# Weights split ahead of time in the first layer, kept in DRAM, and loaded ready made by the attention stage

## The chip, the cores and the metric

One core of a Trainium2 chip runs the kernel. The metric is the device time of one execution in microseconds (us), taken as the median of several runs. Engines are named as in the profile: PE (TensorE, matrix products; PEld its weight loads), DVE (VectorE), ACT (ScalarE), POOL (GpSimd) and SP (SyncE, which issues DMA transfers here). POOL issues DMA transfers as well, on a queue of its own; the accumulating ones must come from it. SBUF is the on-chip memory, PSUM the banks that PE writes to, DRAM the memory outside.

## The reference

Two layers of a decoder on 1024 tokens of width 1024, all in float32:

```
for i in (0, 1):
    h = rmsnorm(x, norm_mixer[i])
    if i == 0: mix = short_conv(h, w_in, conv_w, w_out)          # gated convolution, width 3
    else:      mix = attention(h, w_qkv, gains, sinks, w_o)      # window of 128, 16 query heads, 4 key heads
    x = x + mix
    h = rmsnorm(x, norm_ffn[i])
    x = x + (silu(h @ w_gate) * (h @ w_up)) @ w_down             # channel mixer, inner width 2816
```

The attention takes 128-query blocks against the block's own and the preceding 128 keys, with RMS norms on the heads of queries and keys, a linear distance bias (ALiBi), and one learned sink logit for each head.

## The kernel before, in words

**Products.** A float32 weight is split into two parts, `hi` (the value rounded to the engine's fast format, F32R) and `lo` (the rest). A product of tiles is three matmuls of 128x128 by 128x512: hi by the operand's high part, hi by its low part, lo by its high part. A split is two instructions on a 128x512 piece (a *granule*): a cast that makes `hi` and a subtraction that makes `lo`. The large products also use a Strassen-like scheme with seven products of half the size (k = 0 to 6) in the place of eight. For four of the seven, the weights are sums of quarters of the matrix. These sums are made in DRAM: plain copies on SP's queue fill a DRAM tile (`s4`, called `q_sums`, for the query weights; `s2_...` for the down projection), and a chain of four accumulating DMA transfers on POOL's queue (`added_sums`, line 901) forms the sums, each transfer waiting for the one before.

**The order of the work.** In the channel mixers and the first mixer, a list called `line` holds every instruction with a planned time: `line.at(t, f)` files a step, `line.work` files matmuls that take 0.2265 us each, and at the end all are issued in order of planned time. So the plan sets only the order on each engine; what an instruction waits for, it waits for when the program runs. In the attention stage the order is a string, one letter for each kind of step (`ORDER`), repeated 64 times, once for each pair of heads and block of queries, and `plan(d, f)` files a step d repetitions later.

**The stages, in order of time.** The convolution layer; its channel mixer (`channel_mixer(0, ...)`: gate and up products with 22 units, of which the last 18, the *steady* ones, take 7 x 12 matmuls or about 19 us each, then the down product from `begin` on); the attention layer; its channel mixer. In the first channel mixer's steady part, from about 400 to 743 us, SP loads two 512 KB weight tiles for each unit (WR and WH, lines 1478 and 1482), ACT and DVE split granules 13 us ahead of their use (lines 937 and 938), ACT and DVE empty PSUM banks (lines 1374 to 1436), and POOL's queue carries the stores of the hidden values (`h`, lines 1431 and 1456 to 1458) and the accumulations for the sums that later stages need, planned 9 us apart. SBUF tiles X0 and X2 hold nothing during the steady units.

**The attention layer.** The first 14 granules, for keys and the first pair of query tiles (`first_pairs`), and the values come first. The other 21 granules of query weights are *streamed* during the 64 repetitions: `load_granule(j)` loads 256 KB of raw weights, from `w_q` or, for sums, from `q_sums`; `split_granule(j + 1, pool, pool)` has POOL make both parts; `three(j, p, x)` makes the product (line 2048). Products of four of the seven kinds read operands that were stored in DRAM earlier (`q_ops`), through `load_operand` (512 KB each). Beside this, for each repetition, PE makes scores (line 2257), POOL the distances (line 2272), DVE the row maxima (`mx`, line 2284), ACT the exponents; POOL also splits queries (line 2216), output operands (line 2470) and a few small things. In the tail of this stage the product with the first half of the output weights runs (`w_o`, eight row tiles m, with the first EARLY = 4 blocks of each): its weights are loaded by `Weights.load` and split by ACT and POOL.

Of the kernel before, what the change touches and what calls it, by code (L numbers as in the profile page):

```python
# [15 lines left out]
P = 128  # L16
# [71 lines left out]
def trunk_kernel(ctx: ExitStack, tc: tile.TileContext, xT, small, w_in, w_out, w_q, w_v, w_o, w_gu, w_dn, out):  # L88
# [6 lines left out]
    def slot(tag, shape=(P, D), dtype=F32, bufs=1):  # L95
        uid[0] += 1
        return sb.tile(list(shape), dtype, tag=tag, name=f"{tag}_{uid[0]}", bufs=bufs)
# [737 lines left out]
    q_sums = tc.dram_tile((4, GROUP + 1, P, 5 * P), F32, name="s4")  # L835
    q_ops = tc.dram_tile((4, 4, P, D), F32, name="q_ops")
    xres = [tc.dram_tile((P, T), F32, name=f"xres{m}") for m in range(NK)]
    x_aside = {m: tc.dram_tile((P, T), F32, name=f"x_aside{m}") for m in (NK - 2, NK - 1)}
    first_sums = [tc.dram_tile((4, GROUP, P, 5 * P), F32, name=f"s1_{l}") for l in range(2)]
    down_sums = [[tc.dram_tile((4, P, (PAIRS + 1) * P), F32, name=f"s2_{l}_{u}") for u in range(GROUP)] for l in range(2)]  # L840
    hidden = [[tc.dram_tile((KINDS, 2, P, HALF), F32, name=f"h_{l}_{i}") for i in range(SLOTS)] for l in range(2)]
    lo_half, hi_half = slice(0, HALF), slice(HALF, T)

    class Line:
# [221 lines left out]
    def channel_mixer(layer, next_stage, src_of, operands, raw_tags, extra_tags, keep_tags, slots, begin_with=(), first_w=None, line=None, lead_in=None, before=None, follow=None):  # L1066
# [520 lines left out]
        if layer == 0:  # L1587
            first_added_sums(1, line, begin + 10.0, 18.0)
            for i, (u, n) in enumerate(((0, 2), (2, 2), (KEYS_AS_PAIR, 1))):
                dst = [q_sums[s, u : u + n][:, :, 0 : 4 * P] for s in range(4)]  # L1590
                parts = [w_q[e, u : u + n][:, :, r] for e in (0, 1) for r in (0, 1)]
                added_sums(dst, parts, line, steady_begins + 75.0 * i + 30.0, 9.0)
# [67 lines left out]
    def attention_layer():  # L1660
# [295 lines left out]
        halves_of = (lo_half, hi_half)  # L1956
        seq = [(KEYS_AS_PAIR, k) for k in KEY_ORDER] + [(u, k) for u in range(NK // 2) for k in QUERY_ORDER]
        n_first = 2 * KINDS
        rooms = {}
# [3 lines left out]
        def pair_rooms():  # L1963
            wr = slot("WR", (P, 2, 4 * P), bufs=2)
            rooms["held"] = slot("WR", (P, 2, HALF), bufs=2)
            rooms["spare"] = slot("WH", (P, 2, HALF), F32R, bufs=2)
            rooms["odd"] = slot("WH", bufs=2)
            wl = [slot("WL", (P, 2, 4 * P), F32R, bufs=2) for _ in range(2)]
            g0 = slot("G0", (P, 2, 4 * P))
            rooms["raws"] = [x[:, i] for x in (wr, g0) for i in (0, 1)]  # L1970
            rooms["grans"] = wl + [rooms["spare"], slot("G2", (P, 2, 4 * P), F32R)]
            rooms["banks"] = [bank(f"P{i}") for i in range(3)]

        def raw_room(j):
            return rooms["raws"][j % 4 if j < n_first else j % 2]

        def gran_room(j):
            return rooms["grans"][j % 4 if j < n_first - 1 else 2 if j == n_first - 1 else j % 2]

        def load_granule(j):  # L1980
            if j < len(seq):
                u, k = seq[j]
                src = {0: w_q[0, u][:, 0], 1: w_q[0, u][:, 1], 4: w_q[1, u][:, 1]}
                src = src[k] if k in src else q_sums[SUMS[k], u][:, 0 : 4 * P]
                nc.sync.dma_start(raw_room(j), src)
            elif j == len(seq):
                nc.sync.dma_start(raw_room(j).rearrange("p (k c) -> p k c", c=P), w_o[0][:, 0 : len(early), :])

# [62 lines left out]
        def first_pairs():  # L2051
# [61 lines left out]
            for j in range(n_first):  # L2113
# [31 lines left out]
                if j == 11:  # L2145
                    at(t + 0.75, first.squares0)
                    at(t + 0.8, keep_v, 0, 1)
            for j in range(n_first + 2):
                if j < n_first:
                    t = begins[j - 3 + (j == n_first - 1)] + 0.05 if j > 3 else begin + 14.0 + 2.4 * j  # L2150
                    at(t, split_granule, j, act, pool if j > 10 else dve)
                if j < 6:
                    at(begin + (2.0 + 1.2 * j if j < 4 else 5.5 + 2.4 * j), load_granule, j)
                else:
                    at(begins[j - (6 if j < n_first else 4)] + (0.02 if j <= n_first else 1.0), load_granule, j)
            at(begins[n_first - 1] + 0.05, split_granule, n_first, act, dve)
            at(begins[n_first - 1] + 1.0, split_granule, n_first + 1, act, pool)
            at(begins[n_first - 1] + 1.2, load_granule, n_first + 2)
            for n in range(4):
# [252 lines left out]
        def plan(d, f):  # L2412

            agenda.setdefault(pos["step"] + d, []).append(f)
# [91 lines left out]
        def work_of_pairs():  # L2506
            n = 0
            for j in range(n_first, len(seq)):
                u, k = seq[j]
                plan(0, lambda j=j: split_granule(j + 1, pool, pool) if j > n_first else None)  # L2510
                if j > n_first:
# [24 lines left out]
        with tc.manual_schedule(engines={E.PE, E.Activation, E.DVE, E.Pool, E.SP}):  # L2536
# [24 lines left out]
            for m in range(NK):  # L2561
                acc = Acc()
                work = product(acc, w, o_split, len(early))
                for k in range(len(early)):
                    if m + 1 < NK and k == 0:
                        w_next = Weights()
                        w_next.load(w_o[m + 1][:, 0 : len(early), :], 0, len(early))
                    if m == 2 and k == 0:
# [15 lines left out]
                    step(work, full=(k != REST or m in (2, 5)) and pos["n"] < NU + 3)  # L2584
                    if m + 1 < NK and k in (1, 2):
                        w_next.split(2 * (k - 1), 2, act, pool)
                run(work)
# [126 lines left out]
```

## Time and profile before

| | us |
|---|---|
| median of 3 runs | 1934.55 (1933.93 to 1935.43) |
| profiled execution | 1935.29 |
| its span, first to last instruction | 1933.4 |
| PE busy | 1912.8 |
| DVE, ACT, POOL busy | 1304.0, 898.0, 367.4 |

The clock granted to PE was 0.997 on average. In the profile's rows, `acc` and `P` are PSUM banks, `XS`, `A`, `G`, `WR`, `WH`, `WL` and `X` SBUF tiles, `s` and `h` DRAM tiles; `out<-in` names what an instruction writes and reads, with buffer numbers left out. L901 is a line of the kernel's source; lines of helpers (L937, L938: the two halves of a split) stand for many places. A wait row reads: engine and line that waited, what it waited for, total, number of times, longest.

### The profile page before, as it was taken

What the parts mean: (1) busy time and instruction counts of PE and PEld (TensorE: products, weight loads), DVE (VectorE), ACT (ScalarE), POOL (GpSimd) and SP (SyncE); (2) the same over time, 40 slices, a digit from 0 to 9 for tenths busy, and PEclk for the clock granted to TensorE, in tenths of its full rate; (3) what the DMA queues carried; (4) which work ended last, traced back from release to release, by engine and by line L of the source; (5) the groups of instructions that cost most, each with busy time, mean ns of one, the idle gap of its engine ahead of it and who ended that gap; (6) DMA issues with size and microseconds to landing.
All of it is one profiled execution on the core that took longest, in us unless ns stands there. A gap on an engine that the chain in (4) does not pass through costs nothing.

```text
span 1933.4 us, 25467 instructions
## 1 busy us (share of the span) xinstructions
PE 1912.8 (99%) x8981; PEld 1594.0 (82%) x8981; DVE 1304.0 (67%) x2257; ACT 898.0 (46%) x1762; POOL 367.4 (19%) x504
## 2 busy tenths in 40 slices
PE   9999999999999999999999999999999999999999
PEld 8888888888888888888887788888888888888887
DVE  8997877975665666556765677788665665665543
ACT  5543464623333334445457777655333333344441
POOL 0011231011211100000017888310111111100000
PEclk9999999999999999999999999999999999999999
DMA  8897595388888638986474562242674676468562
GB/s 316 249 256 148 132 250 157 113 272 213 226 249 227 169 120 307 321 251 191 139 255 160 172 209 79 63 171 71 218 216 131 209 187 169 129 235 281 195 229 99
DMA packets 155487, 376.22 MB, mean 195 GB/s; under 512 B 15456, under 2 KB 26848, under 8 KB 155360
## 3 DMA queue, kind: packets, MB, share of 16 engines
q1 hardware_dynamic: 119968, 265.25, 40.4%
q0 software_dynamic: 35248, 109.33, 23.5%
q8 instruction: 70, 1.15, 0.2%
q14 instruction: 57, 0.47, 0.1%
q10 hardware_dynamic: 144, 0.03, 0.0%
HBM read 301.93 MB, written 150.47 MB: 234 GB/s over the span
## 4 chain that ended last, share of the span: by engine, by line
PE 92%; POOL 3%; DVE 1%; ACT 1%; issue 1%; DMA 0%; POOLq 0%; DVEq 0%; ACTq 0%
PE acc L1004 16%; PE acc L1005 16%; PE acc L1007 16%; PE P L1004 10%; PE P L1007 10%; PE P L1005 10%; PE acc L171 2%; PE P L2048 2%; PE acc L2048 2%; POOL G L2216 1%; PE acc L175 1%; PE P L2313 1%; PE acc L1137 1%; PE acc L1139 1%; PE acc L1138 1%
## 5 line engine op out<-in xcount | busy, mean ns | idle before, releaser
L1004 PE MATMUL acc<-XS,G 128*128 128x512 f32 x926 | 360.4, 389 | 0.0
L1007 PE MATMUL acc<-XS,G 128*128 128x512 f32 x926 | 360.3, 389 | 0.0
L1005 PE MATMUL acc<-XS,G 128*128 128x512 f32 x926 | 360.2, 389 | 0.0
L1004 PE MATMUL P<-A,G 128*128 128x512 f32 x550 | 214.2, 389 | 0.4 <-DVE G L547 0.4
L1005 PE MATMUL P<-A,G 128*128 128x512 f32 x550 | 214.0, 389 | 0.0
L1007 PE MATMUL P<-A,G 128*128 128x512 f32 x550 | 214.0, 389 | 0.0
L1005 PEld LDWEIGHTS acc<-XS,G 128*128 128x128 f32 x926 | 173.8, 188 | 36.1
L1004 PEld LDWEIGHTS acc<-XS,G 128*128 128x128 f32 x926 | 173.8, 188 | 36.1
L1007 PEld LDWEIGHTS acc<-XS,G 128*128 128x128 f32 x926 | 173.8, 188 | 36.0
L1004 PE MATMUL acc<-A,G 128*128 128x512 f32 x442 | 172.1, 389 | 0.0
L1007 PE MATMUL acc<-A,G 128*128 128x512 f32 x442 | 172.0, 389 | 0.0
L1005 PE MATMUL acc<-A,G 128*128 128x512 f32 x442 | 171.9, 389 | 0.0
L938 DVE TENSOR_TENSOR G<-WR,G 128x512 fp32r<-128x512 f32 (+1 forms) x216 | 144.2, 668 | 30.0 <-ACT G L937 29.8
L938 DVE TENSOR_TENSOR G<-WL,G 128x512 fp32r<-128x512 f32 x168 | 115.0, 685 | 73.1 <-ACT G L937 73.1
L937 ACT CAST G<-WR 128x512 fp32r<-128x512 f32 (+1 forms) x216 | 130.4, 605 | 59.3 <-PE acc L1007 25.5
L937 ACT CAST G<-WH 128x512 fp32r<-128x512 f32 (+1 forms) x174 | 104.6, 601 | 85.0 <-PE acc L1007 41.8
L1339 ACT ACTIVATE G<-G 128x512 f32<-128x512 f32 x88 | 55.8, 634 | 159.1 <-DVE G L1436 152.9
L938 DVE TENSOR_TENSOR G<-WH,G 128x512 fp32r<-128x512 f32 (+1 forms) x174 | 115.5, 664 | 21.0 <-ACT G L937 20.9
L901 POOL DMA_DIRECT2D s<-s x68 | 60.1, 894 | 364.4 <-DMA s<-s 195.3
L1004 PEld LDWEIGHTS P<-A,G 128*128 128x128 f32 x550 | 103.2, 188 | 22.2 <-DVE G L547 0.8
L1005 PEld LDWEIGHTS P<-A,G 128*128 128x128 f32 x550 | 103.2, 188 | 21.4
L1007 PEld LDWEIGHTS P<-A,G 128*128 128x128 f32 x550 | 103.2, 188 | 21.4
(445 smaller groups left out, 3835.7 us busy)
## 6 DMA issues: line engine op xcount, KB each, us to landing
G<-h SPq DMA_DIRECT2D x70, 512.0 KB, 4.6
s<-in_w_dn SPq DMA_DIRECT2D x32, 704.0 KB, 8.4
h<-X POOLq DMA_DIRECT2D x44, 512.0 KB, 5.3
s<-s POOLq DMA_DIRECT2D x32, 704.0 KB, 7.4
WR<-s SPq DMA_DIRECT2D x79, 256.0 KB, 3.6
WR<-in_w_gu SPq DMA_DIRECT2D x36, 512.0 KB, 5.1
WH<-in_w_gu SPq DMA_DIRECT2D x36, 512.0 KB, 4.9
XS<-q_ops SPq DMA_DIRECT2D x36, 512.0 KB, 5.4
```

Source lines behind the costliest of these rows:

```text
L171: pe.matmul(ps.half(h), wh, xs[:, j, c], start=first and j == 0, stop=False)
L175: pe.matmul(ps.half(h), wl, xs[:, 0, c], start=False, stop=last)
L901: nc.gpsimd.dma_start(dst[to], dst[of], accum_op=ALU.add)
L937: lambda: act.copy(out_hi, raw),
L938: lambda: lo_eng.tensor_tensor(out_lo, raw, plain(out_hi), ALU.subtract),
L1004: pe.matmul(ps, w[:, 0, c], x[:, 0, :], start=start and e == 0, stop=False, skip_group_check=True)
L1005: pe.matmul(ps, w[:, 0, c], x[:, 1, :], start=False, stop=False, skip_group_check=True)
L1007: pe.matmul(ps, w[:, 1, c], x[:, 0, :], start=False, stop=last, skip_group_check=True)
L1137: pe.matmul(ps, hi[:, kc], xs[:, 0, c], start=k == 0, stop=False, skip_group_check=True)
L1138: pe.matmul(ps, hi[:, kc], xs[:, 1, c], start=False, stop=False, skip_group_check=True)
L1339: state["silu"] = act.activation(x, x, AF.Silu)
L2048: pe.matmul(ps, g[:, w, c], x[:, b, :], start=begin and i == 0, stop=end and i == 2, skip_group_check=True)
```

## The change

The 21 streamed granules of query weights and the first halves of the eight row tiles of `w_o` (29 pieces) are no longer split in the attention layer. A new function, `part_ahead`, makes their parts in the first layer's channel mixer: for each piece SP loads 256 KB of raw weights into one half of tile X0, ACT casts and DVE subtracts into tile X2, and POOL's queue stores both parts (512 KB) to a DRAM tile of the piece's own (`parts_q14` to `parts_q34`, `parts_o0` to `parts_o7`). A piece is planned every 10.26 us ((begin - steady_begins - 45) / 29), from steady_begins + 25 on: the load at t, the cast at t + 7.0, the subtraction at t + 7.9, the store at t + 8.7. The pieces of `w_o` come first, then the query weights that need no sum, then those from `q_sums`. There are two raw halves and one tile for the parts. In the attention layer `load_granule` loads 512 KB of ready parts for these granules, into three rooms in turn (two of WL, one of WR) where there were two; `split_granule` is left to the first 14; and the tail loads ready parts of `w_o` into WL and WH in turn.

The core of the diff:

```diff
+    seq = [(KEYS_AS_PAIR, k) for k in KEY_ORDER] + [(u, k) for u in range(NK // 2) for k in QUERY_ORDER]
+    n_first = 2 * KINDS
+    parted = {("q", j): tc.dram_tile((P, 2, 4 * P), F32, name=f"parts_q{j}") for j in range(n_first, len(seq))}
+    parted.update({("o", m): tc.dram_tile((P, 2, 4 * P), F32, name=f"parts_o{m}") for m in range(NK)})
 ...
+    def granule_source(j):
+        u, k = seq[j]
+        src = {0: w_q[0, u][:, 0], 1: w_q[0, u][:, 1], 4: w_q[1, u][:, 1]}
+        return src[k] if k in src else q_sums[SUMS[k], u][:, 0 : 4 * P]
+
+    def part_ahead(line, jobs):
+
+        rooms_ = {}
+
+        def one(n, name, t):
+            it = {}
+
+            def load():
+                if not rooms_:
+                    both = slot("X0", (P, 2, HALF))
+                    rooms_["raw"] = both[:, 0], both[:, 1]
+                    rooms_["out"] = slot("X2", (P, 2, 4 * P), F32R)
+                raw = it["raw"] = rooms_["raw"][n % 2]
+                if name[0] == "q":
+                    nc.sync.dma_start(raw, granule_source(name[1]))
+                else:
+                    nc.sync.dma_start(raw.rearrange("p (k c) -> p k c", c=P), w_o[name[1]][:, 0:EARLY, :])
+
+            def hi():
+                out_ = rooms_["out"]
+                it["steps"] = split_steps(out_[:, 0], out_[:, 1], it["raw"])
+                it["steps"][0]()
+
+            line.at(t, load)
+            line.at(t + 7.0, hi)
+            line.at(t + 7.9, lambda: it["steps"][1]())
+            line.at(t + 8.7, lambda: nc.gpsimd.dma_start(parted[name], plain(rooms_["out"])))
+
+        for n, (name, t) in enumerate(jobs):
+            one(n, name, t)
 ...
+            names = [("o", m) for m in range(NK)]
+            names += [("q", j) for j in range(n_first, len(seq)) if seq[j][1] in (0, 1, 4)]
+            names += [("q", j) for j in range(n_first, len(seq)) if seq[j][1] not in (0, 1, 4)]
+            pace = (begin - steady_begins - 45.0) / len(names)
+            part_ahead(line, [(name, steady_begins + 25.0 + pace * n) for n, name in enumerate(names)])
 ...
+            rooms["later"] = [wl[1], None, wl[0]]
 ...
         def raw_room(j):
-            return rooms["raws"][j % 4 if j < n_first else j % 2]
+            return rooms["raws"][j % 4]
 
         def gran_room(j):
-            return rooms["grans"][j % 4 if j < n_first - 1 else 2 if j == n_first - 1 else j % 2]
+            if j >= n_first:
+                k = (j - n_first) % 3
+                if rooms["later"][k] is None:
+                    rooms["later"][k] = slot("WR", (P, 2, 4 * P), F32R, bufs=2)
+                return rooms["later"][k]
+            return rooms["grans"][j % 4 if j < n_first - 1 else 2]
 
         def load_granule(j):
-            if j < len(seq):
-                u, k = seq[j]
-                src = {0: w_q[0, u][:, 0], 1: w_q[0, u][:, 1], 4: w_q[1, u][:, 1]}
-                src = src[k] if k in src else q_sums[SUMS[k], u][:, 0 : 4 * P]
-                nc.sync.dma_start(raw_room(j), src)
-            elif j == len(seq):
-                nc.sync.dma_start(raw_room(j).rearrange("p (k c) -> p k c", c=P), w_o[0][:, 0 : len(early), :])
+            if j < n_first:
+                nc.sync.dma_start(raw_room(j), granule_source(j))
+            elif j <= len(seq):
+                nc.sync.dma_start(plain(gran_room(j)), parted["q", j] if j < len(seq) else parted["o", 0])
 
         def split_granule(j, hi_eng=dve, lo_eng=pool):
 ...
-            for j in range(n_first + 2):
+            for j in range(n_first + 3):
                 if j < n_first:
                     t = begins[j - 3 + (j == n_first - 1)] + 0.05 if j > 3 else begin + 14.0 + 2.4 * j
                     at(t, split_granule, j, act, pool if j > 10 else dve)
                 if j < 6:
                     at(begin + (2.0 + 1.2 * j if j < 4 else 5.5 + 2.4 * j), load_granule, j)
                 else:
-                    at(begins[j - (6 if j < n_first else 4)] + (0.02 if j <= n_first else 1.0), load_granule, j)
-            at(begins[n_first - 1] + 0.05, split_granule, n_first, act, dve)
-            at(begins[n_first - 1] + 1.0, split_granule, n_first + 1, act, pool)
-            at(begins[n_first - 1] + 1.2, load_granule, n_first + 2)
 ...
-                plan(0, lambda j=j: split_granule(j + 1, pool, pool) if j > n_first else None)
                 if j > n_first:
                     load_granule(j + 2)
 ...
-                        w_next = Weights()
-                        w_next.load(w_o[m + 1][:, 0 : len(early), :], 0, len(early))
+                        g = slot(("WL", "WH")[(m + 1) % 2], (P, 2, 4 * P), F32R, bufs=2)
+                        nc.sync.dma_start(plain(g), parted["o", m + 1])
+                        w_next = SimpleNamespace(hi=g[:, 0], lo=g[:, 1])
 ...
-                    if m + 1 < NK and k in (1, 2):
-                        w_next.split(2 * (k - 1), 2, act, pool)
```

How this moves instructions, at the places of which the prediction speaks. First POOL in the first channel mixer, around the second set of accumulations (`s2_0_1` and `s4`; `h` are the stores of hidden values). Before:

```order
L1431 DMA h_0_2_128<-X4_605_4218 128x512
L901 DMA s2_0_1_119<-s2_0_1_119 128x1408 x2
L1431 DMA h_0_2_128<-X6_622_4355 128x512
L901 DMA s2_0_1_119<-s2_0_1_119 128x1408 x2
L901 DMA s4_104<-s4_104 256x512
L1456 DMA h_0_2_128<-X6_622_4355 128x512
L1457 DMA h_0_2_128<-X5_631_4422 128x2x512
L1458 DMA h_0_2_128<-X7_632_4423 128x2x512
L1431 DMA h_0_2_128<-X1_641_4500 128x512
```

Now:

```order
L1471 DMA h_0_2_157<-X4_607_4276 128x512
L941 DMA s2_0_1_148<-s2_0_1_148 128x1408
L879 DMA parts_o7_134<-X2_538_3725 128x1024
L941 DMA s2_0_1_148<-s2_0_1_148 128x1408
L1471 DMA h_0_2_157<-X6_624_4420 128x512
L941 DMA s2_0_1_148<-s2_0_1_148 128x1408
L879 DMA parts_q14_106<-X2_538_3725 128x1024
L941 DMA s2_0_1_148<-s2_0_1_148 128x1408
L879 DMA parts_q18_110<-X2_538_3725 128x1024
L941 DMA s4_104<-s4_104 256x512
L1496 DMA h_0_2_157<-X6_624_4420 128x512
L1497 DMA h_0_2_157<-X5_633_4490 128x2x512
```

Between the accumulations and the stores of hidden values now stand the stores of the parts, one for each piece.

Next ACT in the same stage, near its beginning (CAST is the high half of a split, COPY and ACTIVATE empty banks or work on what came from them; s1 and s0 belong to one unit and the next). Before:

```order
L1339 ACTIVATE G9_530_3637<-G9_530_3637 128x512
L937 CAST G6_542_3735<-WL_538_3707 128x512
L1416 COPY s1_545_3754<-acc_527_3615 128x512
L937 CAST G7_546_3756<-WL_539_3708 128x512
L1374 COPY G10_547_3773<-acc_544_3750 128x512
L937 CAST G2_548_3775<-WL_538_3707 128x512
L937 CAST G5_551_3794<-WR_543_3740 128x512
L937 CAST G1_553_3814<-WH_532_3648 128x512
L1339 ACTIVATE G9_530_3637<-G9_530_3637 128x512
```

Now:

```order
L1379 ACTIVATE G9_530_3666<-G9_530_3666 128x512
L977 CAST G6_544_3767<-WL_540_3739 128x512
L977 CAST X2_538_3725<-X0_537_3724 128x512
L1456 COPY s1_547_3787<-acc_527_3644 128x512
L977 CAST G7_548_3790<-WL_541_3740 128x512
L1414 COPY G10_549_3809<-acc_546_3783 128x512
L977 CAST G2_550_3811<-WL_540_3739 128x512
L977 CAST G5_553_3830<-WR_545_3772 128x512
L977 CAST G1_555_3850<-WH_532_3677 128x512
L1379 ACTIVATE G9_530_3666<-G9_530_3666 128x512
L977 CAST X2_538_3725<-X0_537_3724 128x512
```

Two casts into X2 have come in, the first right ahead of the copy of a bank into s1.

Last POOL in the attention stage, at the turn from one pair of heads to the next (the 128x64 and 128x128 pieces of `away` are the first distances of a pair, the 64x8x64 rows splits of queries, s1 belongs to the softmax's sums). Before:

```order
L1991 CAST WL_1140_7850<-WR_1136_7846 128x512
L1992 TENSOR_TENSOR WL_1140_7850<-WR_1136_7846,WL_1140_7850 128x512
L2272 TENSOR_TENSOR s0_1190_8384<-cst_1_61,away_1216_8558 128x2x192
L2370 TENSOR_TENSOR den_1207_8503<-den_1207_8503,mx_1204_8479 128x16
L2216 TENSOR_TENSOR G5_1265_8919<-G7_1178_8281,G5_1265_8919 64x8x64
L2269 TENSOR_TENSOR G2_1191_8385<-cst_1_61,away_1258_8861 128x64
L2269 TENSOR_TENSOR G2_1191_8385<-cst_1_61,away_1258_8861 128x128
L1829 COPY s1_1273_8988<-den_1207_8503 128x512
L1991 CAST WL_1141_7851<-WR_1136_7846 128x512
L1992 TENSOR_TENSOR WL_1141_7851<-WR_1136_7846,WL_1141_7851 128x512
L2272 TENSOR_TENSOR G2_1191_8385<-cst_1_61,away_1258_8861 128x2x192
L2272 TENSOR_TENSOR X7_1192_8386<-cst_1_61,away_1258_8861 128x2x192
```

Now, from the same first distances of a pair (that of G2):

```order
L2259 TENSOR_TENSOR G5_1268_9051<-G7_1180_8428,G5_1268_9051 64x8x64
L2315 TENSOR_TENSOR s0_1192_8528<-cst_1_61,away_1219_8698 128x2x192
L2413 TENSOR_TENSOR den_1210_8643<-den_1210_8643,mx_1207_8621 128x16
L2259 TENSOR_TENSOR G5_1268_9051<-G7_1180_8428,G5_1268_9051 64x8x64
L2312 TENSOR_TENSOR G2_1193_8529<-cst_1_61,away_1261_8993 128x64
L2312 TENSOR_TENSOR G2_1193_8529<-cst_1_61,away_1261_8993 128x128
L1874 COPY s1_1276_9118<-den_1210_8643 128x512
L2315 TENSOR_TENSOR G2_1193_8529<-cst_1_61,away_1261_8993 128x2x192
L2315 TENSOR_TENSOR X7_1194_8530<-cst_1_61,away_1261_8993 128x2x192
L1874 COPY s1_1287_9197<-den_1210_8643 128x512
L1974 TENSOR_TENSOR A3_1250_8918<-X6_1168_8311,A1_1249_8917 64x1024
```

The casts and subtractions into WL are gone; distances, splits of queries and the rest stand in the order they had.

More of the change, by code (lines that the diff above doesn't have):

```diff
@@ L1956, in attention_layer @@
         halves_of = (lo_half, hi_half)
-        seq = [(KEYS_AS_PAIR, k) for k in KEY_ORDER] + [(u, k) for u in range(NK // 2) for k in QUERY_ORDER]
-        n_first = 2 * KINDS
         rooms = {}
@@ L2154, in first_pairs @@
                 else:
-                    at(begins[j - (6 if j < n_first else 4)] + (0.02 if j <= n_first else 1.0), load_granule, j)
-            at(begins[n_first - 1] + 0.05, split_granule, n_first, act, dve)
-            at(begins[n_first - 1] + 1.0, split_granule, n_first + 1, act, pool)
-            at(begins[n_first - 1] + 1.2, load_granule, n_first + 2)
+                    at(begins[j - 6] + 0.02 if j < n_first else begins[n_first - 2 + (j > n_first)] + 0.05 + 0.5 * (j - n_first), load_granule, j)
             for n in range(4):
```

## The prediction

> **What bounds the kernel now.** I read the page first: spans, the forty slices, the chain that ended last.
>
> ```profile
> span 1933.4 us, 25467 instructions
> ...
> PE 1912.8 (99%) x8981; PEld 1594.0 (82%) x8981; DVE 1304.0 (67%) x2257; ACT 898.0 (46%) x1762; POOL 367.4 (19%) x504
> ...
> PE 92%; POOL 3%; DVE 1%; ACT 1%; issue 1%; DMA 0%; POOLq 0%; DVEq 0%; ACTq 0%
> ```
>
> TensorE is busy for all but 20.6 us. POOL is busy for 19% of the span and yet holds 3% of the chain, so there is a stretch in which POOL decides. The busy time by stage finds it. The rows are, in order: a quiet moment of the first layer's channel mixer, three parts of that mixer, the attention stage while query weights stream, and its tail.
>
> ```profile
> core 0: us, PE busy (x) PEld busy (x) DVE busy (x) ACT busy (x) POOL busy (x), PEclk, DMA share, GB/s
> 435.00:440.00 5.00, 5.00 (x24) 4.13 (x23) 1.98 (x3) 2.15 (x4) 0.74 (x2) 1.00 0.32 84
> 420.00:573.00 153.00, 153.00 (x676) 126.69 (x676) 92.73 (x145) 52.33 (x96) 27.60 (x37) 1.00 0.85 232
> 573.00:648.00 75.00, 75.00 (x332) 62.10 (x332) 45.28 (x71) 26.16 (x48) 13.77 (x19) 1.00 0.78 204
> 648.00:743.00 95.00, 95.00 (x421) 78.67 (x420) 59.57 (x90) 37.47 (x65) 9.42 (x14) 1.00 0.51 150
> 1016.00:1190.00 174.00, 159.62 (x996) 136.07 (x994) 114.03 (x355) 134.74 (x388) 146.26 (x190) 0.97 0.51 166
> 1190.00:1260.00 70.00, 69.95 (x425) 60.56 (x424) 53.49 (x137) 46.05 (x140) 36.78 (x52) 1.00 0.23 76
> ```
>
> The change moves work from the fifth row, where POOL is 84% busy and TensorE stands for 14.4 us, to the second to fourth, where TensorE never stands but the DMA engines are 85, 78 and 51% busy. Both sides have to be priced. First the attention stage, by who waits for whom:
>
> ```profile
> PE P L2257 <- DVE mx L2284: 5.6, 6, 2.5
> PE acc L2048 <- POOL WL L1991: 3.8, 3, 2.0
> PE acc L171 <- POOL XS L2470: 1.6, 1, 1.6
> PE acc L2048 <- DVE WL L1992: 0.9, 1, 0.9
> ...
> PE acc L2048 <- ACT WL L1991: 0.3, 1, 0.3
> ```
>
> Three of its longest waits are followed by a lower granted clock:
>
> ```profile
> 1076.00:1086.00 10.00, 10.00 (x62) 9.00 (x62) 6.59 (x20) 8.54 (x24) 9.68 (x13) 0.84 0.71 211
> 1096.00:1106.00 10.00, 7.86 (x42) 6.64 (x42) 7.03 (x22) 5.76 (x18) 9.61 (x13) 0.83 0.11 32
> 1146.00:1156.00 10.00, 7.46 (x41) 6.41 (x40) 6.27 (x19) 6.33 (x19) 9.54 (x12) 0.83 0.19 71
> ```
>
> That costs 10 x (0.16 + 0.17 + 0.17) = 5.0 us more. So 14.4 + 5.0 = 19.4 us is all that the attention stage can give back.
>
> **Gain: POOL's splits leave the attention stage.** What goes, from the groups by line in 1016 to 1190:
>
> ```profile
> L1992 POOL TENSOR_TENSOR WL<-WR,WL 128x512 fp32r<-128x512 f32 x21 | 27.3, 1302 | 1.7
> ...
> L1991 POOL CAST WL<-WR 128x512 fp32r<-128x512 f32 x20 | 12.3, 615 | 3.1 <-PE acc L2048 2.6
> ```
>
> POOL loses 27.3 + 12.3 = 39.6 of 146.3 us and falls to 106.7 of 174, or 61%. The waits that name a granule's split (3.8 + 0.9 + 0.3) go outright, and so does most of the one for an output operand behind a split (1.6): 6.6 us. The other 14.4 - 6.6 = 7.8 us are mostly score matmuls that wait for a row maximum, and the maxima wait for POOL's distances, which stand behind splits; I take two thirds, 5.2. Of the three clock drops one follows a split wait and two a maximum wait; I take two thirds of 5.0, 3.4. Against this the first ready-made granules, 512 KB each instead of 256, now start in the same 10 us as four operand loads: 1 us. Sum 6.6 + 5.2 + 3.4 - 1 = 14 us. Ends: 5 (the direct waits alone, less 1.6 for late loads) and 19.4. Elsewhere loads of twice the size are covered: each is issued two granules ahead, and 21 times another 256 KB (0.72 us each, priced below) lift the stage's DMA share from 0.51 only to 0.6. The splits of early output weights gain nothing, because the tail has 0.05 us of idle TensorE.
>
> **Cost: 29 jobs in the mixer.** One starts every 10.26 us from about 426 us: a 256 KB load (SP), a cast (ACT), a subtraction (DVE), a 512 KB store (POOL's queue). The engines' part comes from these groups:
>
> ```profile
> L938 DVE TENSOR_TENSOR G<-WR,G 128x512 fp32r<-128x512 f32 (+1 forms) x216 | 144.2, 668 | 30.0 <-ACT G L937 29.8
> ...
> L937 ACT CAST G<-WR 128x512 fp32r<-128x512 f32 (+1 forms) x216 | 130.4, 605 | 59.3 <-PE acc L1007 25.5
> ```
>
> 29 x 0.605 = 17.5 us on ACT and 29 x 0.668 = 19.4 on DVE, on engines that are 34 and 61% busy there: hidden, cost 0, as long as neither is held up. What could hold them is the DMA side. Queues and landing times from 420 to 573:
>
> ```profile
> q0 software_dynamic: 5438, 17.30, 52.7%
> q1 hardware_dynamic: 5528, 18.10, 32.3%
> ...
> s<-s POOLq DMA_DIRECT2D x8, 704.0 KB, 7.9
> ...
> s<-s POOLq DMA_DIRECT2D x8, 512.0 KB, 10.3
> h<-X POOLq DMA_DIRECT2D x8, 512.0 KB, 7.2
> ```
>
> POOL's queue (q0) already runs a chain of 16 accumulating transfers there: 8 x 7.9 + 8 x 10.3 = 146 of 153 us. Each waits for the one before, and POOL waits with it:
>
> ```profile
> 463.52 0.96 POOL L901 DMA_DIRECT2D s<-s  x1 [0.37 <-issue]
> 477.85 0.90 POOL L901 DMA_DIRECT2D s<-s  x1 [13.36 <-DMA s<-s]
> ```
>
> And it is served in order. A 256 KB store with nothing ahead lands in 2.4 us (issued at 439.3), the same store right behind two accumulations in 13.6 (at 448.4). The third row is a 512 KB store alone (at 641.4):
>
> ```profile
> h<-X POOLq DMA_DIRECT2D x1, 256.0 KB, 2.4
> ```
> ```profile
> h<-X POOLq DMA_DIRECT2D x1, 256.0 KB, 13.6
> ```
> ```profile
> h<-X POOLq DMA_DIRECT2D x1, 512.0 KB, 3.3
> ```
>
> Price of a job in time of all 16 engines: q1 moves 18.10 MB in 0.323 x 153 = 49.4 us, 0.366 MB/us, so the load is 0.72 us; the store lies between 0.524 / 0.366 = 1.43 and twice the step from 2.4 to 3.3, 1.8. A job is 2.15 to 2.5 us. From 420 to 573 the engines have 0.85 x 153 = 130 us of work and get 14.3 jobs more, 31 to 36: 161 to 166 us in 153, so 8 to 13 late. From 573 to 648, 0.78 x 75 = 58.5 plus 16 to 18 is just full. After 648 it drains. The lower end, 8, supposes that every gap can be filled. It can't: with one accumulation in flight the share is 0.32 (435 to 440). If half of the 23 idle us of the first part stay idle, the queue is 11 later: upper end 24. I take 17, nearer the middle than the ends.
>
> Now who waits. All jobs share one output tile (X2), so job n+1's cast on ACT waits until job n's store has landed; planned, it stands 8.56 us behind that store's issue, and a store takes 7.2: 1.4 us of slack. While ACT stands, the copies of TensorE's results stand behind it, and DVE behind those. The shortest thread back to TensorE, at 452 us:
>
> ```profile
> 451.75 0.59 ACT L1416 COPY s<-acc 128x512 f32<-128x512 f32 x1 [3.29 <-PE acc L1007]
> ```
> ```profile
> 452.38 0.69 DVE L1385 TENSOR_TENSOR s<-P,s 128x512 f32<-128x512 f32 x1 [1.22 <-ACT s L1416]
> ```
> ```profile
> 457.00 0.39 PE L1004 MATMUL P<-A,G 128*128 128x512 f32 x1
> ```
>
> DVE is done with the bank at 453.07 and TensorE writes to it again at 457.00: 3.9 us of slack, once in each 19 us. Weight splits have more (the kernel plans them 13 us ahead). So 17 us of lateness cost TensorE 17 - 1.4 - 3.9 = 11.7, say 11.5 us, in a few stalls: a lateness that grows to 17 by 573 passes 5.3 about 470, so they lie between 470 and 640. Once it has lost that, the rest of the program, casts too, comes that much later, and the lateness no longer bites. Ends: 8 - 5.3 = 3 and 24 - 5.3 = 19.
>
> **Sum.** -14 + 11.5 = -2.5 us. The profiled execution took 1935.29 us around its span of 1933.4, 0.74 above the median of the three runs, 1934.55, and I set the sum against the median: 1932.0. About 0.2%, 3.9 us, is what a measurement of this kernel can tell from no change, so this is a forecast near the border.
>
> **Rivals.**
> 1. The queue keeps up. If the engines fill their gaps and the lateness stays under 5.3 us, TensorE loses 0 to 3 and the kernel takes 1934.55 - 14 = 1920.5 to 1923.5. For it: no wait of TensorE in the mixer today although accumulations come up to 14 us apart instead of the planned 9. Against: 161 us of work in 153. The Trainium skill speaks for it (DMA: Bandwidth & Descriptors, section on the anatomy of one DMA): about 2.0 us fixed and bytes / 436e3 us beside it, which makes 3.2 us of a 512 KB store, where the trace has 3.3. By its variable part alone a job would be an estimated 1.2 + 0.6 = 1.8 us, 156 in 153 up to 573 and 72 in 75 after, with no loss left: 1920.5. Its price is for one transfer by itself; the 7.2 us of the same store in this stage is why I stay with the rows.
> 2. Slower: the mixer loses more than the attention stage gains. Place: ACT's cast behind the store. It decides from a lateness of 14 + 5.3 = 19.3 us. At the upper end, 24, the loss is 18.7 and the time 1939; SP adds to it, because a part load that waits for its tile (X0) holds the unit weights queued behind it, up to 1945.
> 3. The attention stage has a second bound near by. ACT is busy for 134.7 of 174 us, 84% of 160. If the maxima stay late, the gain is 5 and the time 1934.55 - 5 + 11.5 = 1941.
>
> **Chances.** Forecast 0.44, of which 0.18 falls below -3.9 us, 0.22 within, 0.04 above; rival 1, 0.22 (faster); rival 2, 0.22 (slower); rival 3, 0.12 (0.04 within, 0.08 slower). Faster 0.40, same 0.26, slower 0.34. Forecast's own range: 1925 to 1938. Range for 8 in 10: 1921 (rival 1) to 1944 (rival 2).
>
> **What would show it.** In the mixer: casts into X2 on ACT that wait for a DMA store, accumulations later than in the rows above by 10 to 20 us around 600, and 8 to 15 us of idle TensorE between 470 and 650. In the attention stage: no wait for WL, POOL near 65%, idle TensorE under 5 us, no 10 us with a clock under 0.9. I am wrong if the mixer's rows still show TensorE busy throughout (then rival 1), or if the maxima's waits remain (rival 3).

## The result, and the profile after

The changed kernel takes 1947.47 us (median of 4 runs, 1942.50 to 1950.54), the kernel before 1934.24 beside it: a ratio of 1.0065, 95% interval 1.0043 to 1.0087. It is 13.2 us slower. The forecast was 1932, and its range ended at 1944. The profiled execution is the shortest of the four, 1942.50 us with a span of 1940.7; the other three had granted clocks of 0.994 to 0.996 against its 0.997. What is read from the trace is therefore the mildest form of the loss.

The page of the profile:

```profile
span 1940.7 us, 25490 instructions
...
PE 1912.4 (99%) x8981; PEld 1593.1 (82%) x8981; DVE 1320.5 (68%) x2285; ACT 907.9 (47%) x1775; POOL 335.1 (17%) x478
...
PE 85%; issue 6%; DMA 3%; ACT 2%; DVE 2%; POOL 2%; SPq 0%; POOLq 0%; DVEq 0%; ACTq 0%
```

TensorE's busy time is what it was (1912.8). Its share of the chain fell from 92 to 85%, and the shares of "issue" (a wait with no releaser in the profile) and of DMA rose from 1 to 6 and from 0 to 3%. The same five stretches as in the prediction, three of the mixer and two of the attention stage (the latter begins some 16 us later now):

```profile
420.00:573.00 153.00, 145.45 (x627) 118.89 (x626) 87.82 (x139) 53.74 (x99) 31.04 (x45) 0.98 0.95 271
573.00:648.00 75.00, 70.05 (x307) 57.00 (x306) 49.35 (x79) 29.71 (x55) 16.74 (x25) 1.00 0.96 290
648.00:743.00 95.00, 95.00 (x421) 78.67 (x420) 64.12 (x102) 37.79 (x69) 18.07 (x28) 1.00 0.74 221
...
1016.00:1190.00 174.00, 164.82 (x1041) 142.16 (x1039) 119.14 (x355) 137.51 (x389) 106.21 (x148) 0.99 0.63 212
1190.00:1260.00 70.00, 68.75 (x431) 59.91 (x430) 53.37 (x144) 44.32 (x137) 31.91 (x46) 1.00 0.20 61
```

In the mixer TensorE stands for 7.55 + 4.95 = 12.5 us, where it stood for none; in the two rows of the attention stage for 9.2 + 1.25 = 10.4 instead of 14.4 (a wait of 1.2 us for an output operand has moved from the fourth row into the fifth). How far the whole program fell behind shows on one group of matmuls at the start of the attention stage (columns: least, median and greatest duration in ns, then the first and the last start), of before and of after:

```profile
L2048 PE MATMUL P<-XS,WL x36: 389/389/397, 976.8 to 990.2; 128*128 128x512 f32 x36
```
```profile
L2094 PE MATMUL P<-XS,WL x36: 389/389/397, 993.3 to 1006.7; 128*128 128x512 f32 x36
```

993.3 - 976.8 = 16.5 us lost by the end of the mixer. (The changed kernel entered it 0.9 us ahead: the first store of hidden values is issued at 393.6 instead of 394.5. So the mixer itself took 17.4.) The spans differ by 7.3, so from there on 9.2 came back. TensorE's waits in the mixer, both of them for ACT's copies of full banks:

```profile
PE acc L1044 <- ACT s L1456: 7.1, 3, 4.9
PE acc L1044 <- ACT G L1422: 5.4, 4, 3.0
```

And what ACT itself waited for in the mixer, at the casts of the jobs (total, times, longest):

```profile
ACT X L977 <- issue: 45.6, 9, 12.1
...
ACT X L977 <- DMA parts_q<-X: 15.7, 4, 8.5
ACT X L977 <- DMA parts_o<-X: 7.9, 2, 7.0
```

The longest stall, step by step. POOL issues job 10's store at 546.33, 5.3 us after that job's cast (541.06): stores of hidden values stand ahead of it in POOL's order, and one of them waits 3.00 us for DVE. The store lands 9.6 us later, at 555.97. Job 11's cast, and behind it the copy of a bank, stand on ACT until then, and TensorE stands for 4.85 us. In the order POOL, landing, ACT, TensorE, and last TensorE's clock after it:

```profile
545.06 0.73 POOL L1498 DMA_DIRECT2D h<-X  x1 [3.00 <-DVE G L1418]
545.78 0.56 POOL L1471 DMA_DIRECT2D h<-X  x1
546.33 0.55 POOL L879 DMA_DIRECT2D parts_q<-X  x1
```
```profile
parts_q<-X POOLq DMA_DIRECT2D x1, 512.0 KB, 9.6
```
```profile
541.06 0.62 ACT L977 CAST X<-X 128x512 fp32r<-128x512 f32 x1 [6.07 <-issue]
...
556.03 0.62 ACT L977 CAST X<-X 128x512 fp32r<-128x512 f32 x1 [8.46 <-DMA parts_q<-X]
556.56 0.58 ACT L1456 COPY s<-acc 128x512 f32<-128x512 f32 x1
```
```profile
557.19 0.80 PE L1044 MATMUL acc<-XS,G 128*128 128x512 f32 x1 [4.85 <-ACT s L1456]
```
```profile
557.00:567.00 10.00, 9.81 (x31) 7.88 (x32) 4.24 (x7) 2.18 (x5) 2.05 (x3) 0.70 1.05 281
```

The clock of 0.70 over 10 us costs another 10 x 0.30 = 3 us. The next cast, at 571.32, has "issue" as its releaser, yet it begins 0.06 us after a store's landing (issued at 560.83, landed 10.43 us later). The same holds for all nine casts with this releaser: each begins 0.06 to 0.07 us after the landing of the store before it, so they are the same wait.

In the attention stage the waits for WL are gone. Two new ones have come in ahead of what is left of those for maxima:

```profile
PE P L2300 <- DVE mx L2327: 3.4, 7, 0.9
PE acc L2094 <- DVE A L1867: 2.1, 1, 2.1
PE P L2300 <- DVE G L2259: 1.5, 1, 1.5
```

### The profile page after: what moved, and what is told of

Its sections match the earlier page's. It is cut to its first block, busy times and chain, and to the rows that moved or that the text cites. A ratio compares the mean times of both kernels' runs of the same rounds, so it can differ in the third digit from the quotient of the medians.

```text
span 1940.7 us, 25490 instructions
## 1 busy us (share of the span) xinstructions
PE 1912.4 (99%) x8981; PEld 1593.1 (82%) x8981; DVE 1320.5 (68%) x2285; ACT 907.9 (47%) x1775; POOL 335.1 (17%) x478
## 4 chain that ended last, share of the span: by engine, by line
PE 85%; issue 6%; DMA 3%; ACT 2%; DVE 2%; POOL 2%; SPq 0%; POOLq 0%; DVEq 0%; ACTq 0%
PE acc L1044 15%; PE acc L1045 15%; PE acc L1047 15%; PE P L1044 8%; PE P L1045 8%; PE P L1047 8%; PE acc L171 3%; PE P L2094 2%; PE acc L2094 2%; PE acc L175 1%; PE P L2356 1%; PE acc L1177 1%; PE acc L1179 1%; PE acc L1178 1%; PE P L1725 1%
```

## The experiments

All times are medians of the runs, each beside runs of the kernel before on the same chip (1934.92 to 1935.08).

| | what it is | us | ratio to before, 95% interval |
|---|---|---|---|
| e1 | the 29 jobs alone | 1954.48 | 1.0101 (1.0088 to 1.0115) |
| e2 | the attention stage's part alone | 1927.77 | 0.9961 (0.9949 to 0.9974) |
| e3 | changed, two output tiles | 1935.90 | 1.0000 (0.9991 to 1.0009) |
| e4 | the jobs' DMA alone | 1935.23 | 1.0001 (0.9993 to 1.0010) |
| e5 | e2, first streamed product in its old place | 1920.55 | 0.9924 (0.9911 to 0.9936) |
| e6 | changed, stores issued by ACT | 1927.45 | 0.9959 (0.9945 to 0.9972) |
| e7 | changed, 22 jobs instead of 29 | 1934.19 | 0.9993 (0.9984 to 1.0002) |
| e8 | e3, e5 and e7 together | 1921.13 | 0.9928 (0.9916 to 0.9941) |
| e9 | changed, old place as in e5 | 1941.34 | 1.0028 (1.0018 to 1.0038) |
| e10 | e5 and e6 together, 29 jobs | 1920.61 | 0.9924 (0.9912 to 0.9936) |

**e1 and e2: the two halves by themselves.** For e1, `part_ahead` and its call are added to the kernel before. For e2:

```diff
-            names = [("o", m) for m in range(NK)]
 ...
-            part_ahead(line, [(name, steady_begins + 25.0 + pace * n) for n, name in enumerate(names)])
+            names = [("o", 0), ("o", 1), ("q", n_first), ("q", n_first + 1)]
+            part_ahead(line, [(name, begin - 90.0 + 18.0 * n) for n, name in enumerate(names)])
 ...
-                nc.sync.dma_start(plain(gran_room(j)), parted["q", j] if j < len(seq) else parted["o", 0])
+                nc.sync.dma_start(plain(gran_room(j)), parted["q", n_first + j % 2] if j < len(seq) else parted["o", 0])
 ...
```

> The kernel before with the 29 jobs of the first channel mixer added, the attention stage left as before (it splits for itself, and the stored parts are not read). In the profiled run of the changed kernel TensorE fell 17.3 us behind in the mixer and won 8.8 us back in the attention stage, and the median over its runs was 13.2 us above the kernel before, so this one should be slower by 17 to 22 us: 1951 to 1957 us. Both theories of the loss (ACT's casts behind the one output tile; the DMA engines full) say so. If it comes out under 1945, the loss in the mixer is not what makes the changed kernel slow, and the attention stage lost more than the profiled run shows.

> The attention stage of the changed kernel, with 4 of the 29 jobs in the mixer, put in its last 90 us, 18 us apart; the 21 granules are then loaded from two of the stored tiles in turn and the early output weights from the other two, so each load has its size and place and the products have wrong weights. Mixer loss at most 1 us. Theory: the attention stage gains 8.8 us, whatever the mixer does, so about 1925.5 us (1924 to 1927). Rival: the gain of the profiled run was cut by what the mixer's delay left behind, and alone it is the 14 us that I forecast: about 1920.5.

e2 (and e5, which builds on it) leaves out 25 of the 29 jobs and loads the four stored pieces again and again, so its transfers have the size and place of the change and its products the wrong weights.

e1 is 19.6 us slower than the kernel before, e2 7.2 faster (0.8 us less than the lower end that I expected); 19.6 - 7.2 = 12.4, close to the 13.2 of the whole change. So the halves add up, and both terms of my sum were too favourable: 11.5 stood for the 19.6, 14 for the 7.2. These are 8.1 + 6.8 = 14.9 of the 15.5 us between forecast and result. That the mixer cuts the attention stage's gain (the rival of e2) is out.

**e4: the jobs' DMA without their casts.** In e1's kernel, the cast and subtraction are planned only for the first job:

```diff
-            line.at(t + 7.0, hi)
-            line.at(t + 7.9, lambda: it["steps"][1]())
+            if n == 0:
+                line.at(t + 7.0, hi)
+                line.at(t + 7.9, lambda: it["steps"][1]())
```

> The kernel before with the 29 raw loads and the 29 stores of the jobs, but a cast and a subtraction for the first of them alone; the output tile is stored 29 times as it is, and the attention stage is as before. All the DMA work of the jobs, none of the waits of ACT for it. Theory one (ACT stands behind the store): TensorE loses 0 to 4 us, 1934 to 1938 us, with accumulations and stores of hidden values as late as in the changed kernel. Rival (the DMA side itself): 10 us or more, 1944 and above.

It takes the time of the kernel before. The three stretches of the mixer, and TensorE's only wait there:

```profile
420.00:573.00 153.00, 153.00 (x677) 126.69 (x676) 93.14 (x146) 52.89 (x97) 29.45 (x43) 1.00 0.96 279
573.00:648.00 75.00, 74.15 (x328) 61.08 (x327) 44.41 (x71) 26.18 (x48) 17.73 (x26) 1.00 0.97 287
648.00:743.00 95.00, 95.00 (x421) 78.66 (x420) 60.33 (x91) 37.64 (x66) 18.06 (x28) 1.00 0.83 246
```
```profile
PE P L1052 <- DVE s L1433: 0.9, 1, 0.9
```

The DMA engines are as busy as in the changed kernel (0.96, 0.97, 0.83 against 0.95, 0.96, 0.74), and the accumulations come later still (the pair issued at 595.1 before comes at 615.0 in the changed kernel and at 622.8 here), but TensorE hardly notices. So full DMA engines cost next to nothing here by themselves; what costs is an engine in the chain that waits for them. e4 also leaves out ACT's and DVE's added work; e6, below, keeps it and loses nothing in the mixer, so that isn't the cost either.

**e3: a second output tile.** The raw weights go into the low half of the tile that will hold the parts, and X0 and X2 take turns:

```diff
-                    both = slot("X0", (P, 2, HALF))
-                    rooms_["raw"] = both[:, 0], both[:, 1]
-                    rooms_["out"] = slot("X2", (P, 2, 4 * P), F32R)
-                raw = it["raw"] = rooms_["raw"][n % 2]
+                    rooms_["out"] = [slot(tag, (P, 2, 4 * P), F32R) for tag in ("X0", "X2")]
+                raw = it["raw"] = plain(rooms_["out"][n % 2][:, 1])
 ...
```

> The changed kernel with two output tiles for the jobs instead of one, in the same SBUF (the raw weights are loaded into the low half of the tile that will hold the parts, X0 and X2 in turn, and the subtraction writes over them). The DMA work is the same. Theory one (the loss is ACT standing at a cast until the store before has left the only output tile, a loop of 2 us from cast to issue and 6 to 10 us to landing, against a pace of 10.26): the loss in the mixer falls from 17 us to 0 to 4, and the time is 1926 to 1930. Rival (the DMA engines and POOL's queue are full, and any way of adding these transfers costs it): the loss stays above 10 us, and the time is 1936 or more.

1935.90 lies between the two, at the edge of the rival's 1936. Against e2, with the same attention stage, the mixer still loses 8.1 us. The trace shows one stall of TensorE there, of 4.6 us, and ahead of it this wait of ACT:

```profile
571.10 0.62 ACT L975 CAST X<-X 128x512 fp32r<-128x512 f32 x1 [9.41 <-DMA X<-in_w_q]
```

A cast no longer waits for the store before it, but its raw load now does: with raw and parts in one tile the load for job 13 was issued at 564.10, right after the store of job 11 had landed. The tile was part of the cause; with this layout 8.1 of the 19.6 us only moved from ACT's wait for a store to its wait for a load behind a store.

**e6: the stores issued by ACT.**

```diff
-            line.at(t + 8.7, lambda: nc.gpsimd.dma_start(parted[name], plain(rooms_["out"])))
+            line.at(t + 9.5, lambda: nc.scalar.dma_start(parted[name], plain(rooms_["out"])))
```

> The changed kernel with the 29 stores of parts issued by ACT on its own queue, right before the next cast, instead of by POOL. One output tile as before. Theory (a store lands late because it stands in POOL's queue behind accumulations, and POOL itself comes to its issue late): the loop from cast to landing falls under the pace of 10.26 us, the loss in the mixer to 0 to 4 us and the time to 1928 to 1932. Rival (a store of 512 KB takes 7 us there on any queue, since the 16 DMA engines are shared): the cast waits as before, the loss stays above 10 us, 1938 or more.

The edit also files the store 0.8 us later in the plan. The time, 1927.45, equals e2's 1927.77 and is 0.55 below what I expected, so the mixer loses nothing now (TensorE is busy for 153.00 of 153 and 75.00 of 75 us). But my reason was only half right. The landing times of the stores (least, median, greatest), of the changed kernel and of e6:

```profile
DMA to landing us min/median/max: 2.9/7.5/11.1
```
```profile
DMA to landing us min/median/max: 2.6/7.0/10.3
```

A store takes about 7 us on either queue, as the rival said. What went is, for the greater part, POOL's lateness in issuing it. Over the first 20 jobs the issue comes 2.97 us after the cast on average in the changed kernel, at most 7.95, and 2.08 in e6, at most 4.19; cast, issue and landing together take 10.9 us on average and up to 16.7 there, 9.4 and 13.4 here. ACT's waits at casts:

```profile
ACT X L977 <- DMA parts_q<-X: 28.2, 11, 5.5
...
ACT X L977 <- DMA parts_o<-X: 3.1, 2, 2.0
```

31.3 us of waits remain, the longest of 5.5, and none reaches TensorE in the mixer. In the changed kernel it was 69.2, with four of 7.0 to 12.1 us. Length alone doesn't decide, though. Two casts of the changed kernel:

```profile
571.32 0.62 ACT L977 CAST X<-X 128x512 fp32r<-128x512 f32 x1 [12.15 <-issue]
...
580.35 0.62 ACT L977 CAST X<-X 128x512 fp32r<-128x512 f32 x1 [3.29 <-DMA parts_q<-X]
```

After the first TensorE stood for 0.22 us (until 574.04), after the second for 1.72 (until 581.51). Each time it waited for the copy of a bank that stands on ACT behind the cast; so it also counts when TensorE needs that bank.

**e7: fewer jobs, further apart.** `names` begins with `("o", 0)` alone, and the tail loads and splits the other seven pieces as before.

> The changed kernel with 22 jobs instead of 29 (the 21 streamed granules and the first row tile of the output weights; the other seven are loaded raw and split in the tail, as before), one every 13.5 us instead of 10.26, all else as it was. Theory (a loop through the one output tile takes 10 to 15 us, so a pace of 10.26 lets it fall behind and 13.5 mostly doesn't): loss in the mixer 2 to 7 us instead of 17 to 20, time 1929 to 1935. Rival (each job costs TensorE a fixed 0.68 us, 19.6 / 29, wherever it stands): 22 x 0.68 = 15 us, time 1942 or more.

1934.19, so the mixer loses 1934.19 - 1927.77 = 6.4 us with 22 jobs instead of 19.6 with 29, as expected: no fixed price for each job. Two stalls of 2.5 and 2.9 us are left.

**e5 and e9: the place of the first streamed product.** This came out of the trace of after. The wait for `A L1867` (2.1 us) belongs to the first streamed granule's product, and it stands elsewhere on TensorE than before. Order of instructions now, with the third from last product of the first granules (`P_1146`) and the streamed one (`acc_8566`):

```
L2094 MATMUL P_1146_8001<-XS_1108_7671,G_1145_8000 128x512 x2
L2094 MATMUL acc_8566<-XS_1104_7650,WL_7998 128x512 x3
L2094 MATMUL acc_8566<-XS_1109_7684,WL_7998 128x512 x3
L2094 MATMUL acc_8566<-XS_1116_7722,WL_7998 128x512 x3
L2094 MATMUL acc_8566<-XS_1120_7757,WL_7998 128x512 x2
L2094 MATMUL P_1146_8001<-XS_1108_7671,G_1145_8000 128x512
```

Before, all 12 matmuls of the streamed product stood behind that product and the two after it. No line of the diff moves them: the two parts of the attention layer are ordered by hand each, but the first steps of the second may be let in among the last of the first when the weights they need are there, and ready-made weights are there earlier. That is how I read it; no run shows why the order changed, only what it costs. e5 puts them back in e2's kernel, e9 in the changed one:

```diff
-                pe.matmul(ps, g[:, w, c], x[:, b, :], start=begin and i == 0, stop=end and i == 2, skip_group_check=True)
+                op = pe.matmul(ps, g[:, w, c], x[:, b, :], start=begin and i == 0, stop=end and i == 2, skip_group_check=True)
+                if j < n_first:
+                    state["last of first"] = op
+                elif j == n_first and p == 0 and i == 0:
+                    issue_behind(op, state["last of first"], "order of the products")
```

> The kernel of e2 (attention stage with parts from DRAM, 4 jobs in the mixer) with one dependency more: the first matmul of the first streamed granule is put behind the last matmul of the 14 first granules. In the changed kernel and in e2 the order had let 11 of its 12 matmuls come before the last product of the first granules, where they waited 2.13 us for a bank. Theory: that order cost the attention stage 3.5 to 5 us (TensorE's lag grew by 3.5 there in the changed kernel, by 5.0 in e2, before it fell); so 1922.5 to 1924.5. Rival: the waits there come from late loads or from the values and stay in any order: 1927.8, the time of e2.

> The changed kernel with the order of the first streamed product kept, and nothing else. If the two losses add up, it is 7.2 us (e2 less e5) under the changed kernel's 1947.5: 1940 (1938 to 1943), still slower than before by the mixer's loss less the 14.4 us of the attention stage. If the late mixer changes what the order costs, it stays at 1945 or more.

e5 gains 14.5 us on the kernel before, 7.2 more than e2; e9 is 6.1 under the changed kernel by the medians, though its 11 runs spread from 1935.45 to 1945.73. The same two stretches of 10 us, in e2 and in e5:

```profile
1010.00:1020.00 10.00, 7.87 (x40) 6.28 (x38) 3.08 (x6) 3.52 (x7) 1.76 (x6) 1.00 0.33 117
1020.00:1030.00 10.00, 8.46 (x44) 6.86 (x43) 5.47 (x15) 7.91 (x17) 2.86 (x4) 1.00 0.43 130
```
```profile
1010.00:1020.00 10.00, 10.00 (x53) 8.49 (x52) 4.88 (x12) 6.43 (x11) 1.79 (x6) 1.00 0.42 137
1020.00:1030.00 10.00, 10.00 (x51) 8.38 (x50) 7.36 (x21) 8.68 (x23) 7.86 (x7) 1.00 0.79 277
```

2.13 + 1.54 = 3.67 us of standing in e2 are gone in e5. In the changed kernel DVE waits for the product that was overtaken, and ACT's and POOL's work on the first queries comes behind DVE:

```profile
1036.63 0.69 DVE L2078 TENSOR_TENSOR G<-P,WR 128x512 f32<-128x512 f32 x1 [5.15 <-PE P L2094]
```

So they too start later in e2 (DVE is busy for 3.08 us in the first row against 4.88, POOL for 2.86 in the second against 7.86); the first maxima are late after that (0.95 us more), and the clock falls: 0.83 over the ten us from 1030, 1.00 in e5. I had expected 3.5 to 5 of it; it was 7.2. The whole stage in e5, and what is left there of the waits for maxima:

```profile
1016.00:1190.00 174.00, 167.75 (x1083) 145.88 (x1082) 126.83 (x390) 142.96 (x417) 118.59 (x165) 0.99 0.62 210
```
```profile
PE P L2301 <- DVE mx L2328: 2.5, 6, 0.6
```

**e8 and e10: both causes removed.**

> 22 jobs 13.5 us apart, two output tiles in turn, and the order of the first streamed product kept: e7, e3 and e5 together. If the three theories hold, the mixer loses 0 to 2 us and the attention stage gains what e5 gains: 1922.5 to 1926.5, faster than both kernels. If the loss of e3 (7.5 us in one wait for a raw load that stood behind a late store) comes back with the wider pace, 1930 or more.

> All 29 jobs at the pace of the changed kernel, stores issued by ACT (e6), order kept (e5). If both work, e6 less 7.2 us: 1920.3 (1919 to 1922), as fast as e8 with its 22 jobs and two tiles. It also tells whether splitting the other seven row tiles of the output weights ahead is worth anything: I expect nothing beyond 1 us against e8, since the tail where they were split had no idle TensorE.

e10 comes out where expected, e8 at 1.4 us under the lower end of what I expected; they are about 14 us faster than the kernel before and 26 faster than the changed one. e8 has fewer jobs, two tiles and POOL's stores; e10 all 29 jobs, one tile and ACT's stores. They are half a us apart, so splitting the seven further pieces of the output weights ahead gains nothing that this measurement can tell (the two differ in tiles and queue as well; TensorE is busy from 420 to 648 us throughout in both). The attention stage of e10:

```profile
1016.00:1190.00 174.00, 167.21 (x1085) 144.84 (x1084) 127.31 (x391) 143.00 (x417) 118.92 (x166) 1.00 0.62 210
```

TensorE stands for 6.8 us of it, at the full clock.

## Why the prediction was wrong, point by point

- **What bounds the kernel** was read rightly: the attention stage had some 14 us to give, and the mixer was where it could be lost.
- **The gain of the attention stage**, 14 us (6.6 + 5.2 + 3.4 - 1), is what e5 shows in sum: 14.5. That the sum fits so well is partly luck. From 1016 to 1190 TensorE stands for 8.1 us less in e5 than before (6.25 instead of 14.4), where 6.6 + 5.2 - 1 = 10.8 were forecast. WL's waits are gone and those for maxima fell from 5.6 to 2.5 us, but the wait for an output operand, counted as won with 1.6, is still 1.6. The other 6 us come from TensorE's busy time, 1906.4 us instead of 1912.8. The clock, 0.99 from 1016 to 1190 where it was 0.97, is 0.02 x 174 = 3.5 of that, as forecast; what the rest is, no run shows.
- **The step that failed there** is that I took the order on TensorE to be the one before: the part on the change shows ACT and POOL, not TensorE. The order now in force lost 7.2 us (e2 less e5), so the changed kernel had half of this gain. The 1 us for the first late loads stood where this should have stood; the waits there were for a bank and for queries, not for loads. Two signs that I had named failed with it: TensorE's idle time in the stage was 10.4 us, not under 5, and its clock was 0.83 from 1174 to 1184.
- **"ACT and DVE work hidden, DMA full"**: DMA share 0.95, 0.96, 0.74 and a store of 7.5 us (I used 7.2) as forecast. e4 shows that this load alone costs next to nothing.
- **The loss in the mixer**: place and mechanism were right (ACT's cast behind the store from the one output tile, copies of banks behind it, TensorE behind those, between 469 and 637 us). The slack of 1.4 + 3.9 = 5.3 us isn't shown: ACT begins to wait only when the 1.4 are used up, and what a wait costs doesn't follow its length (7.0 us cost 1.9, 12.15 cost 0.22, 3.29 cost 1.72). The 12.5 us of standing lie in the forecast 8 to 15. The second step that failed is what the standing costs, which I put at 11.5 and e1 shows as 19.6. After a stall the clock falls for some us, which I had priced in the attention stage (three times) and left out here: 16.5 us of delay for 12.5 of standing in the profiled run, and 3 us of the difference are the clock's. (e1's profiled run, its slowest with 1957.93, stands for 8.0 + 6.6 = 14.6 us from 420 to 648, with a clock of 0.99 and 0.95.) Nor did I ask what comes of it from run to run: the runs of the changed kernel spread over 8 us, those of e8 over 0.5.
- **How the loss was derived** also holds only in part. I let lateness grow once to 17 us and subtracted one slack. It is a loop instead: cast, issue by POOL, landing, next cast, over the first 20 jobs 10.9 us on average and up to 16.7, at a pace of 10.26. And I took POOL to issue on plan, 1.7 us after the cast; it came 2.97 after it on average and up to 7.95. e7 (13.5 us apart), e6 (earlier issue) and e3 (two tiles) each cut the loss by this reading.
- **Rivals.** The second, slower, happened in sign and place: the mixer's 19.6 us are more than the 14.5 that the attention stage can give, and with the old order on TensorE (e9) the kernel takes 1941.34, within its 1939 to 1945. What the order cost on top no rival had. The first (the queue keeps up, 1920.5 to 1923.5) was wrong of this kernel: in the mixer the store took a median of 7.5 us. The Trainium skill, which spoke for it (DMA: Bandwidth & Descriptors, the anatomy of one DMA), gives an estimated 3.2 us by its formula; the measurement decides here. The third (ACT as the second bound in the attention stage) is out: e10 does the stage's work with ACT at 143.00 of 174.

Why POOL came late to issue the stores shows in its order in the profiled run. Of the first 20 stores five are issued over 4 us after their cast. Ahead of three of them (jobs 2, 10 and 17) stand stores of hidden values that wait for DVE, up to 5.21 us, and ahead of two (jobs 8 and 11) an accumulation that waits for the one before, up to 5.12. What stays open are POOL's waits with "issue" as releaser, up to 8.2 us, and why the order on TensorE changed.

## What to carry to other kernels

Work hidden on idle engines still costs when one of its steps waits on an engine that empties TensorE's banks: price the loop through the single buffer (issue delay, landing, reuse) against the pace, and ask of each wait which bank's copy stands behind it and when TensorE needs that bank, instead of going by the share of busy time. When a change makes an operand ready earlier, read the order of every engine again, the bound one first: here work that was let in early cost half of the gain, and one dependency brought it back. And a stall's price is its length and, often, a slower clock after it, on the side of the loss as well as of the gain.

## What the runs showed of the hardware

DMA engines at a share of 0.95 to 0.99 from 420 to 648 us delayed TensorE by less than 1 us (0.9 in e4, 0 in e6). A 512 KB store took about 7 us there on either queue (a median of 7.0 on ACT's, 7.5 on POOL's). The mixers of the profiled changed kernel, e1, e3, e7 and e9 show ten waits of TensorE of over 2.5 us; after nine the clock was 0.70 to 0.85 over the next 10 us (0.70 after the one of 4.85), after one, of 3.02 us at 636, it was 1.00. Three shorter ones in the changed kernel (1.9, 1.7 and 0.6 us) were followed by 1.00. A drop can also come without such a wait: in e5 the clock is 0.83 from 1150 to 1160, and the last wait before it, at 1136, is 0.65 us long.
